# Windowed attention on one core: v of the last unit goes back to its usual place in the load order, and the first transfer is cut in two

## The chip, the cores and the metric

The kernel runs on one core of one Trainium2 chip. The metric is the device time of one execution in microseconds (us). A profiled execution also has a span, from its first to its last instruction, about 1.8 us shorter than its time.

## The reference

Attention inside windows of 64 rows, float32 in and out, 4 x 4096 rows of 1536 columns:

```python
q_w, k_w, v_w = (x.reshape(B, S // 64, 64, D) for x in (q, k, v))
logits = np.einsum('bnwd,bnud->bnwu', q_w, k_w) * D ** -0.5
attn = softmax(logits)                       # over the last axis
out = np.einsum('bnwu,bnud->bnwd', attn, v_w)
```

Each element of q, k and v is read once and each output written once: 301.99 MB in, 100.66 MB out.

## The kernel before

The rows are worked off in 32 units (`N = 32`) of 512 rows, numbered 0 to 31 here. A unit is four transfers of 3.146 MB on the HBM side: q, k and v in (cast from float32 to float16 on the way, so 1.573 MB land) and the result out. GpSimd issues them all, except the first load of q and the second half of the last store, which SyncE issues. Each operand is loaded into a landing buffer (`ql`, `kl`, two for v), copied by GpSimd to the buffer that TensorE reads (`q16`, `k16`, `v16`), and its landing buffer is then reloaded:

```python
def hand_over(src, dst, d, u, m, g):
    gp.wait_ge(d, 16 * u)                       # the load has landed
    gp.wait_ge(m, copies[0] // 3 + 1)           # the unit before no longer reads dst
    gp.tensor_copy(out=dst..., in_=src...).then_inc(c_l, 1)
    copies[0] += 1
    gp.wait_ge(c_l, copies[0])
    gp.sem_inc(g, 1)                            # TensorE may go on
```

The start, cut:

```python
raw = rows(qf, 0, SLOTS, SLOTS).rearrange("p h (r d) -> p (h r) d", d=D)
for sl, s in ((slice(0, 1), d_r0), (slice(1, 2), d_r1), (slice(2, SLOTS), d_r2)):
    nc.sync.dma_start(out=outs[0][:, sl, :], in_=raw[:, sl, :]).then_inc(s, 16)
...
nc.gpsimd.wait_ge(d_r0, 16)                     # holds back the loads behind it
nc.gpsimd.affine_select(out=ident[:, :], ...)   # the identity for the transposes
load("k", 0, k16, d_k0)
load("v", 0, v16, d_v0)
for i in range(SLOTS):                          # SLOTS = 4
    nc.gpsimd.wait_ge((d_r0, d_r1, d_r2, d_r2)[i], 16)
    nc.gpsimd.tensor_copy(out=q16[:, i, :], in_=outs[0][:, i, :])
    if i == 1:
        load("q", 1, ql, d_q)
load("k", 1, kl, d_k)
for u in range(1, NV + 1):                      # NV = 2
    load("v", u, vls[u % NV], d_v[u % NV])
```

GpSimd's main loop and the end of the program:

```python
for u in range(1, N):
    hand_over(ql, q16, d_q, u, m_q, g_q)
    if u + 1 < N:
        load("q", u + 1, ql, d_q)
    hand_over(kl, k16, d_k, u, m_k, g_k)
    if u + 1 < N:
        load("k", u + 1, kl, d_k)
    for what in {N - 3: "", N - 2: "-v"}.get(u, "s"):
        if what == "v":
            load("v", N - 1, vls[(N - 1) % NV], d_v[(N - 1) % NV])
        else:
            gp.wait_ge(m_q, u + 1)
            store(u - 2 if what == "-" else u - 1)
    if u == N - 2:
        store(u - 1)
    hand_over(vls[u % NV], v16, d_v[u % NV], (u + u % NV) // NV, m_v, g_v)
    if u + NV < N - 1:
        load("v", u + NV, vls[u % NV], d_v[u % NV])

base, o = (N - 1) * UR, outs[(N - 1) % NO]
for h, (eng, c) in enumerate(((gp, 1), (sy, 3))):   # the last store, in halves
    for a in range(2):
        eng.wait_ge(n_e[a], c)
    eng.dma_start(out=rows(of, base + R * P * h, R, R), in_=slots(o, R * h, R * h + R, R)).then_inc(d_l[h], 16)
gp.drain()
...                                             # SyncE waits for every store, then:
sy.sem_inc(done, 1)
gp.wait_ge(done, 1)
gp.sem_clear(range(lo, hi + 1))
```

So store 28 and v31 are held back until k31 has been issued, and the order at the end is q31, k31, store 28, v31, store 29, store 30, last store.

The softmax here doesn't subtract the row's maximum and nothing guards it: scores larger than these inputs give would overflow.

Of the kernel before, what the change touches and what calls it, by code (L numbers as in the profile page):

```python
# [17 lines left out]
def kernel(  # L18
# [13 lines left out]
    nc = tc.nc  # L32
    PE, DVE, ACT = (getattr(mybir.EngineType, e) for e in ("PE", "DVE", "Activation"))
    B, S, D = q.shape
    DC = D // (2 * P)
    NJ = D // 512
    SLOTS, R, H = 4, 2, 2
    UR = P * SLOTS
    N = B * S // UR
# [3 lines left out]
    def sb(name, shape, dtype):  # L43
        return ctx.enter_context(nc.sbuf_tensor(name, shape, dtype))
# [6 lines left out]
    def sem(name):  # L51
        sems.append(nc.alloc_semaphore(name))
        return sems[-1]
# [6 lines left out]
    NV = 2  # L60
    vls = [sb(f"vl{i}", [P, SLOTS, D], FP16) for i in range(NV)]
# [3 lines left out]
    outs = [sb(f"out{i}", [P, SLOTS, D], FP32) for i in range(NO)]  # L65
# [7 lines left out]
    ops = [ps(f"o{j}", [P, 512]) for j in range(NJ)]  # L73
    sp = ps("sp", [P, 4])

    d_r0, d_r1, d_r2, d_q, d_k, d_k0, d_v0 = (
        sem(n) for n in ("d_r0", "d_r1", "d_r2", "d_q", "d_k", "d_k0", "d_v0")
    )
    d_v = [sem(f"d_v{i + 1}") for i in range(NV)]
    d_o = [sem(f"d_o{i}") for i in range(NO)]  # L80
# [11 lines left out]
    m_q, m_k, m_v = (sem(n) for n in ("m_q", "m_k", "m_v"))  # L92
# [6 lines left out]
    def rows(x, row0, n, r):  # L99
        return x[row0 : row0 + P * n].rearrange("(h p r) d -> p h (r d)", p=P, r=r)  # L100

    def slots(t, lo, hi, r):
        return t[:, lo:hi, :].rearrange("p (h r) d -> p h (r d)", r=r)

    def load(name, u, dst, s):
        src = {"q": qf, "k": kf, "v": vf}[name]
        r = R if name == "v" else SLOTS
        nc.gpsimd.dma_start(
            out=slots(dst, 0, SLOTS, r), in_=rows(src, u * UR, SLOTS, r)
        ).then_inc(s, 16)  # L110
# [169 lines left out]
    def store(u):  # L280
        nc.gpsimd.dma_start(
            out=rows(of, u * UR, SLOTS, R), in_=slots(outs[u % NO], 0, SLOTS, R)
        ).then_inc(d_o[u % NO], 16)
# [3 lines left out]
    def hand_over(src, dst, d, u, m, g):  # L287

        gp = nc.gpsimd
        gp.wait_ge(d, 16 * u)  # L290
        gp.wait_ge(m, copies[0] // 3 + 1)
        gp.tensor_copy(  # L292
            out=dst[:, :, :].bitcast(FP32), in_=src[:, :, :].bitcast(FP32)
        ).then_inc(c_l, 1)
        copies[0] += 1
        gp.wait_ge(c_l, copies[0])
        gp.sem_inc(g, 1)

    with tc.tile_critical(no_gpsimd_drain=True):

        raw = rows(qf, 0, SLOTS, SLOTS).rearrange("p h (r d) -> p (h r) d", d=D)
        for sl, s in ((slice(0, 1), d_r0), (slice(1, 2), d_r1), (slice(2, SLOTS), d_r2)):
            nc.sync.dma_start(out=outs[0][:, sl, :], in_=raw[:, sl, :]).then_inc(s, 16)
        nc.vector.memset(ident[:, :], 0.0).then_inc(i_d, 1)
        nc.gpsimd.wait_ge(i_d, 1)
        nc.gpsimd.wait_ge(d_r0, 16)
        nc.gpsimd.affine_select(
            out=ident[:, :], in_=ident[:, :], compare_op=mybir.AluOpType.not_equal,
            fill=1.0, base=0, pattern=[[-1, P]], channel_multiplier=1,
        ).then_inc(i_p, 1)  # L310
        load("k", 0, k16, d_k0)
        load("v", 0, v16, d_v0)

        for i in range(SLOTS):
            nc.gpsimd.wait_ge((d_r0, d_r1, d_r2, d_r2)[i], 16)
            nc.gpsimd.tensor_copy(out=q16[:, i, :], in_=outs[0][:, i, :]).then_inc(c_q, 1)
            if i == 1:
                load("q", 1, ql, d_q)
        load("k", 1, kl, d_k)
        for u in range(1, NV + 1):  # L320
            load("v", u, vls[u % NV], d_v[u % NV])

        nc.vector.memset(ones[:, :], 1.0).then_inc(i_d, 1)
        nc.vector.memset(zeros[:, :], 0.0).then_inc(i_d, 1)
        for et in ets:
            nc.vector.memset(et[:, :, :, :], 0.0).then_inc(i_d, 1)
        nc.scalar.wait_ge(i_d, 5)
        nc.scalar.activation(zeros[:, 3:4], zeros[:, 0:1], EXP, bias=zeros[:, 0:1], scale=1.0)

        with nc.Fori(0, N, engines=OrderedEngineSet([PE]), head_slot={PE: 0}):  # L330
            tensor_unit()
        assert N % NO == 2
        for eng, unit in ((DVE, vector_unit), (ACT, scalar_unit)):
            with nc.Fori(0, N // NO, engines=OrderedEngineSet([eng]), head_slot={eng: 0}):
                for u in range(NO):
                    unit(u)
            for u in range(N - 2, N):
                unit(u)

        sy = nc.sync  # L340
        for j in range(NJ):
            for n in (2, 3):
                sy.sem_inc(f_o[j][n], 1)
        for a in range(2):
            sy.sem_inc(fr[a], NO)
        sy.wait_ge(i_p, 1)
        sy.wait_ge(i_d, 5)
        sy.wait_ge(c_q, SLOTS)
        sy.sem_inc(g_q, 1)
        sy.sem_inc(g_k, 1)._wait_ge(d_k0, 16)  # L350
        sy.sem_inc(g_v, 1)._wait_ge(d_v0, 16)
        for u in range(NO, N):
            sy.wait_ge(d_o[u % NO], 16 * (u // NO))
            for a in range(2):
                sy.sem_inc(fr[a], 1)

        gp = nc.gpsimd
# [5 lines that stand above are left out]
            if u + 1 < N:  # L363
                load("k", u + 1, kl, d_k)

            for what in {N - 3: "", N - 2: "-v"}.get(u, "s"):
                if what == "v":
                    load("v", N - 1, vls[(N - 1) % NV], d_v[(N - 1) % NV])
                else:
                    gp.wait_ge(m_q, u + 1)  # L370
                    store(u - 2 if what == "-" else u - 1)
            if u == N - 2:
                store(u - 1)
            hand_over(vls[u % NV], v16, d_v[u % NV], (u + u % NV) // NV, m_v, g_v)
            if u + NV < N - 1:
                load("v", u + NV, vls[u % NV], d_v[u % NV])

        base, o = (N - 1) * UR, outs[(N - 1) % NO]
        for h, (eng, c) in enumerate(((gp, 1), (sy, 3))):
            for a in range(2):  # L380
                eng.wait_ge(n_e[a], c)
            eng.dma_start(
                out=rows(of, base + R * P * h, R, R), in_=slots(o, R * h, R * h + R, R)
            ).then_inc(d_l[h], 16)
        gp.drain()
        for i in range(NO):
            last = max(u for u in range(N - 1) if u % NO == i)
            sy.wait_ge(d_o[i], 16 * (last // NO + 1))
        for i in range(2):
            sy.wait_ge(d_l[i], 16)  # L390
        sy.sem_inc(done, 1)
        gp.wait_ge(done, 1)
        lo, hi = min(s.num for s in sems), max(s.num for s in sems)
        assert hi - lo + 1 == len(sems)
        gp.sem_clear(range(lo, hi + 1))
# [30 lines left out]
```

## Time and profile before

| what | before |
|---|---|
| time, median of 4 runs (range) | 947.35 us (946.81 to 947.80) |
| span of the profiled execution | 946.4 us |
| one steady round of four transfers | 29.16 us, 431.5 GB/s |
| HBM traffic at that rate | 933.1 us |
| busy PE, DVE, ACT, GpSimd | 69%, 30%, 35%, 36% |
| DMA engines | full in 39 of the 40 slices |

(The prediction was made from the first three of these runs, median 947.6.) A transfer adds 16 to its semaphore, one step for each DMA engine, so the trace's semaphore records give 16 landing times for each. For the transfers around the gap, in us from the start of the span (worked out from the semaphore records of the kernel before):

```
transfer    issued    first engine done   last engine done
q30         855.98    878.8               881.7
k30         863.32    886.1               889.0
q31         885.13    894.6               896.3
k31         892.41    902.8               906.3
store 28    892.93    910.6               913.6
```

The engines are up to 3.5 us apart. A copy on GpSimd, and everything that waits for a transfer, sees only the last.

### The profile page before, as it was taken

How to read it: one execution, taken by the hardware profiler on the slowest of the kernel's cores; microseconds unless marked ns; L12 is line 12 of the kernel's file. 1: busy time of each engine (PE TensorE's matmuls, PEld its weight loads, DVE VectorE, ACT ScalarE, POOL GpSimd, SP SyncE). 2: the span in 40 equal slices, each digit the busy share in tenths (PEclk: the TensorE clock that was granted, in tenths of full speed). 3: DMA queues.
4: the chain of work that ended last, by engine and by line, in shares of the span. 5: the costliest groups of instructions: out<-in, count | busy, mean ns of one | idle time of the engine just before them, and what ended most of it. 6: DMA issues, size and time to landing. Idle time of an engine off the chain costs nothing. (4 is left out here: it accounts for less than half of the span.)

```text
span 946.4 us, 11421 instructions
## 1 busy us (share of the span) xinstructions
PE 651.0 (69%) x4096; PEld 419.8 (44%) x3456; DVE 279.7 (30%) x453; ACT 332.8 (35%) x642; POOL 341.5 (36%) x229
## 2 busy tenths in 40 slices
PE   2776866768667676667777667866768666777682
PEld 2544543445534345434554344543435533445450
DVE  1333223332233231333313323223322233232331
ACT  1433323333334342333423334323333234343252
POOL 4323343233442334423344323343233442333520
PEclk9989777897878887798878789878898879797897
DMA  9999999999999999999999999999999999999997
GB/s 250 216 229 270 283 281 282 242 257 283 281 280 258 243 282 282 278 270 236 278 282 280 279 238 265 282 280 282 249 251 283 283 281 264 238 279 283 197 315 321
DMA packets 26940, 253.35 MB, mean 268 GB/s; under 512 B 2096, under 2 KB 2096, under 8 KB 10544
## 3 DMA queue, kind: packets, MB, share of 16 engines
q0 software_dynamic: 26352, 248.52, 100.0%
q1 hardware_dynamic: 576, 4.72, 1.3%
q14 instruction: 10, 0.08, 0.0%
q8 instruction: 2, 0.03, 0.0%
HBM read 301.99 MB, written 100.66 MB: 425 GB/s over the span
## 5 line engine op out<-in xcount | busy, mean ns | idle before, releaser
L147 PE MATMUL tp<-ident,q 128*128 128x128 f32 x768 | 165.0, 384 | 185.6 <-PEq L213 172.7
L147 PEld LDWEIGHTS tp<-ident,q 128*128 128x128 f32 x768 | 131.2, 200 | 239.4 <-issue 236.8
L292 POOL COPY q<-ql 128x3072 f32<-128x3072 f32 x31 | 85.0, 2743 | 395.7 <-DMA ql<-in_q_dram 395.5
L159 PE MATMUL lt<-xq,xk 128*128 128x256 f16 x1536 | 210.2, 288 | 0.0
L147 PE MATMUL tp<-ident,k 128*128 128x128 f32 x768 | 136.3, 317 | 67.3 <-PEq L213 54.5
L159 PEld LDWEIGHTS lt<-xq,xk 128*128 128x128 f16 x1536 | 156.8, 102 | 30.4
L222 ACT COPY xq<-tp 128x512 f32<-128x512 f32 x96 | 60.2, 627 | 291.2 <-ACTq L213 291.2
L147 PEld LDWEIGHTS tp<-ident,k 128*128 128x128 f32 x768 | 105.1, 163 | 86.3 <-issue 83.9
L222 DVE COPY xq<-tp 128x512 f32<-128x512 f32 x96 | 66.4, 692 | 254.7 <-DVEq L213 254.7
L222 ACT COPY xk<-tp 128x512 f32<-128x512 f32 x96 | 59.8, 623 | 228.6 <-ACTq L213 228.6
L222 DVE COPY xk<-tp 128x512 f32<-128x512 f32 x96 | 66.5, 693 | 198.6 <-DVEq L213 198.6
L292 POOL COPY k<-kl 128x3072 f32<-128x3072 f32 x31 | 85.3, 2751 | 110.5 <-DMA kl<-in_k_dram 110.5
L264 ACT ACTIVATE et<-lt,zeros 32x128 f16<-32x128 f32 x256 | 92.0, 359 | 39.4 <-ACTq L213 36.1
L188 PEld LDWEIGHTS <-et 128*128 128x128 f16 x384 | 30.2, 97 | 152.7 <-issue 116.7
L115 PE MATMUL o<-v,et 128*128 128x512 f16 x384 | 93.3, 379 | 0.0
L251 DVE TENSOR_SCALAR out<-o,rs 128x512 f32<-128x512 f32 x128 | 90.2, 747 | 7.7
L292 POOL COPY v<-vl 128x3072 f32<-128x3072 f32 x31 | 85.5, 2758 | 10.4 <-DMA vl<-in_v_dram 10.4
L115 PE MATMUL tp<-v,et 128*128 128x512 f16 x256 | 75.8, 377 | 0.0
L241 DVE RECIPROCAL rs<-sp 128x2 f32<-128x2 f32 x64 | 10.6, 166 | 162.6 <-DVEq L213 162.4
L275 ACT ACTIVATE out<-tp,rs 128x512 f32<-128x512 f32 x64 | 44.0, 688 | 37.2 <-ACTq L213 31.3
L251 DVE TENSOR_SCALAR out<-tp,rs 128x512 f32<-128x512 f32 x64 | 48.1, 751 | 26.2 <-DVEq L213 26.2
L115 PE MATMUL lt<-v,et 128*128 128x512 f16 x128 | 48.3, 377 | 0.0
(22 smaller groups left out, 201.2 us busy)
## 6 DMA issues: line engine op xcount, KB each, us to landing
out_dram<-out POOLq DMA_DIRECT2D x31, 3072.0 KB, 32.5
ql<-in_q_dram POOLq DMA_DIRECT2D x31, 1536.0 KB, 25.8
kl<-in_k_dram POOLq DMA_DIRECT2D x31, 1536.0 KB, 25.8
vl<-in_v_dram POOLq DMA_DIRECT2D x31, 1536.0 KB, 35.7
out<-in_q_dram SPq DMA_DIRECT2D x2, 768.0 KB, 6.5
out<-in_q_dram SPq DMA_DIRECT2D x1, 1536.0 KB, 11.2
k<-in_k_dram POOLq DMA_DIRECT2D x1, 1536.0 KB, 12.2
v<-in_v_dram POOLq DMA_DIRECT2D x1, 1536.0 KB, 18.8
```

The costliest lines, as they stand in the source:

```text
L115: return nc.tensor.add_instruction(mybir.InstMatmult(name=nc.get_next_instruction_name(), engine=PE, ins=[low(rhs), low(w)], outs=[low(o)] ...
L147: ins = nc.tensor.transpose(tps[g % 2][:, r, j, :], pairs[:, c * P : (c + 1) * P], ident[:, :])
L159: ins = nc.tensor.matmul(lts[h][:, r, :, :], lhsT=halves(xk, c)[:, r, h, :, w], rhs=halves(xq, c)[:, :, h, :, w], start=(c == 0 and w == 0 ...
L188: ld = nc.tensor.ldweights(w)
L222: copy(out=dst, in_=tps[g % 2][:, :, :, :]).then_inc(f_c[g % 4], 1)
L241: ve.reciprocal(out=rs[:, n : n + R], in_=sp[:, n : n + R]).then_inc(n_d, 1)
L251: ins = ve.tensor_scalar_mul(scaled(u, n, j), bank(n, j), scalar1=rs[:, n : n + 1])
L264: ins = sc.activation(ets[h][s, :, :, s], lts[h][s, :, :, s], EXP, bias=zeros[s, 0:1], scale=scale)
L275: ins = sc.activation(scaled(u, n, j), bank(n, j), COPY, bias=0.0, scale=rs[:, n : n + 1])
L292: gp.tensor_copy(out=dst[:, :, :].bitcast(FP32), in_=src[:, :, :].bitcast(FP32)).then_inc(c_l, 1)
```

## The change

At the end, only store 28 is held back; v31 is loaded right after v of unit 29 has been handed over. At the start, the first slot of q comes in two halves.

```diff
...
-        for sl, s in ((slice(0, 1), d_r0), (slice(1, 2), d_r1), (slice(2, SLOTS), d_r2)):
-            nc.sync.dma_start(out=outs[0][:, sl, :], in_=raw[:, sl, :]).then_inc(s, 16)
+        for lo, hi, c0, c1, s in (
+            (0, 1, 0, D // 2, d_r0), (0, 1, D // 2, D, d_r1), (1, 2, 0, D, d_r2), (2, SLOTS, 0, D, d_r3)
+        ):
+            nc.sync.dma_start(
+                out=outs[0][:, lo:hi, c0:c1], in_=raw[:, lo:hi, c0:c1]
+            ).then_inc(s, 16)
...
-            nc.gpsimd.wait_ge((d_r0, d_r1, d_r2, d_r2)[i], 16)
+            nc.gpsimd.wait_ge((d_r1, d_r2, d_r3, d_r3)[i], 16)
...
-            for what in {N - 3: "", N - 2: "-v"}.get(u, "s"):
-                if what == "v":
-                    load("v", N - 1, vls[(N - 1) % NV], d_v[(N - 1) % NV])
-                else:
-                    gp.wait_ge(m_q, u + 1)
-                    store(u - 2 if what == "-" else u - 1)
-            if u == N - 2:
+            if u != N - 3:
+                gp.wait_ge(m_q, u + 1)
+                if u == N - 2:
+                    store(u - 2)
                 store(u - 1)
             hand_over(vls[u % NV], v16, d_v[u % NV], (u + u % NV) // NV, m_v, g_v)
-            if u + NV < N - 1:
+            if u + NV < N:
                 load("v", u + NV, vls[u % NV], d_v[u % NV])
```

The order at the end becomes v31, q31, k31, store 28, store 29, store 30, last store.

More of the change, by code (lines that the diff above doesn't have):

```diff
@@ L74 @@
     sp = ps("sp", [P, 4])
-    d_r0, d_r1, d_r2, d_q, d_k, d_k0, d_v0 = (
-        sem(n) for n in ("d_r0", "d_r1", "d_r2", "d_q", "d_k", "d_k0", "d_v0")
+    d_r0, d_r1, d_r2, d_r3, d_q, d_k, d_k0, d_v0 = (
+        sem(n) for n in ("d_r0", "d_r1", "d_r2", "d_r3", "d_q", "d_k", "d_k0", "d_v0")
     )
```

## The prediction

> **What bounds the kernel now.** I read the page first (busy shares, the 40 slices, bytes), then the timeline of GpSimd, which issues nearly all transfers, then the rate in 3 us windows at both ends, then landing times by tile. The page:
>
> ```profile
> span 946.4 us, 11421 instructions
> PE 651.0 (69%) x4096; PEld 419.8 (44%) x3456; DVE 279.7 (30%) x453; ACT 332.8 (35%) x642; POOL 341.5 (36%) x229
> DMA  9999999999999999999999999999999999999997
> HBM read 301.99 MB, written 100.66 MB: 425 GB/s over the span
> ```
>
> No compute engine is near full; the 16 DMA engines are, in every slice but the last. (The GB/s row counts a load that casts f32 to f16 at its f16 size, so about 215 there is a full-speed load and about 430 a full-speed store.) GpSimd's copies of q repeat at 735.98, 765.14 and 794.31 us, every 29.16 us, and one round moves four transfers (q, k, v, store) of 3.146 MB on the HBM side: 7.29 us each, 431.5 GB/s. So 402.65 MB need 933.1 us, and a change can win only part of the other 13.3: DMA time lost at the start, lost in between, or after the last byte. The diff touches start and end only. GpSimd's timeline of the end:
>
> ```profile
> 863.86 2.76 POOL L292 COPY v<-vl 128x3072 f32<-128x3072 f32 x1
> ...
> 885.13 0.53 POOL L108 DMA_DIRECT2D ql<-in_q_dram  x1 [0.58 <-POOL q L292]
> 889.07 2.75 POOL L292 COPY k<-kl 128x3072 f32<-128x3072 f32 x1 [3.41 <-DMA kl<-in_k_dram]
> 892.41 0.53 POOL L108 DMA_DIRECT2D kl<-in_k_dram  x1 [0.58 <-POOL k L292]
> 892.93 0.71 POOL L281 DMA_DIRECT2D out_dram<-out  x1
> 893.63 0.72 POOL L108 DMA_DIRECT2D vl<-in_v_dram  x1
> 894.35 0.71 POOL L281 DMA_DIRECT2D out_dram<-out  x1
> ...
> 906.36 2.75 POOL L292 COPY k<-kl 128x3072 f32<-128x3072 f32 x1 [5.57 <-DMA kl<-in_k_dram]
> 912.53 0.72 POOL L281 DMA_DIRECT2D out_dram<-out  x1 [3.42 <-ACTq L220]
> 920.93 2.74 POOL L292 COPY v<-vl 128x3072 f32<-128x3072 f32 x1 [7.69 <-DMA vl<-in_v_dram]
> 929.57 0.55 POOL L382 DMA_DIRECT2D out_dram<-out  x1 [5.89 <-ACT out L275]
> ```
>
> I number units 0 to 31. At 863.86 v of unit 29 is handed over and its buffer is free, but nothing is issued. The queue holds only q30 and k30, and when q31 goes in at 885.13, only the rest of k30 is ahead of it. The same stretch in 3 us windows (last column GB/s, before it the DMA share), against a full one ahead and behind:
>
> ```profile
> 875.00:878.00 3.00, 3.00 (x20) 0.51 (x6) 2.50 (x5) 2.03 (x5) 0.00 (x0) 1.00 1.04 221
> 884.00:887.00 3.00, 1.98 (x9) 1.64 (x10) 0.69 (x1) 0.05 (x1) 1.08 (x2) 0.50 1.05 197
> 887.00:890.00 3.00, 2.87 (x14) 2.31 (x15) 0.69 (x1) 1.20 (x2) 0.93 (x1) 0.59 0.91 188
> 893.00:896.00 3.00, 2.45 (x23) 2.06 (x21) 1.33 (x2) 0.76 (x2) 3.00 (x4) 1.00 0.96 168
> 896.00:899.00 3.00, 3.00 (x29) 2.69 (x28) 0.69 (x1) 0.87 (x2) 2.77 (x2) 1.00 0.92 175
> 932.00:935.00 3.00, 0.00 (x0) 0.00 (x0) 0.00 (x0) 0.00 (x0) 0.00 (x0) 0.81 1.00 426
> 941.00:944.00 3.00, 0.00 (x0) 0.00 (x0) 0.00 (x0) 0.00 (x0) 0.00 (x0) 0.50 0.03 12
> ```
>
> Loads ran at 168 to 197 instead of about 215: summed over one-microsecond windows from 885 to 902 the mean is 188, so 17 x (1 - 188/215) = about 2.1 us lost. From 920 to 940 all is full. The landing times of the q load show the thin queue:
>
> ```profile
> DMA to landing us min/median/max: 11.2/25.8/26.4
> ```
>
> A load normally lands 25.8 us after issue, 3.5 transfers, so 2.5 were ahead of it. The 11.2 is q31: half a transfer ahead of it.
>
> **What the Trainium skill says.** The page "DMA: Bandwidth & Descriptors", section "Specifications", gives a fabric ceiling of 435 GB/s; the steady rounds run at 431.5, so they have nothing more to give. Its section "Issuing engines are not separate DMA queues" says that transfers of all issuers share the same 16 engines and interleave: reordering creates no bandwidth, it can only fill gaps. Its section "Why a DMA increments its semaphore by 16 and not by 1" says the 16 engines finish independently: a transfer lands with its slowest engine, and an engine that is ahead idles when nothing is queued behind. The profile gives only the mean of the engines; the dips at 885 and 894 fit, but don't prove it. "Anatomy of one DMA" puts a fixed 2.0 us beside the data time, most of it write receipt; here the rate falls at about 940.5 and the last store lands at 929.57 + 13.3 (median of its issue row) = 942.9, so it agrees.
>
> **The change, part by part.** (1) End, removed and moved: v31 leaves its place between two stores and is issued as usual, right after the hand-over of v29, at about 867. Store 28 and store 29 go out behind k31 at about 893, store 30 as before. No instruction or byte is added here. From the landing of k30 at 889.07, with both orders at 7.29 us each:
> Before, from the landings: q31 896.3, k31 906.3, store 28 913.6, v31 920.8, store 29 928.3, store 30 936.4, last unit 942.9. That is 53.8 us for seven transfers; 7 x 7.29 = 51.0, so 2.8 us were lost, and 10.0 - 7.3 = 2.7 of them lie at k31, where the windows dip.
> After: v31 896.4, q31 903.7, k31 911.0, store 28 918.2, store 29 925.5, store 30 932.8, last unit 940.1. A whole transfer (v31) now stands between k30 and q31, and no dip should stay. Best case -2.8 us.
>
> (2) What this does to the last unit. k31 lands 4.7 us later, v31 24 us earlier. The 7.7 us wait for v31 vanishes and k31 becomes the gate. From unit 29: k lands 859.97, its transposes start 863.03, the third of four output rows is ready at 878.0 (14.97 later), the last at 879.5. So the first half of the last store is issued at 911.0 + 3.1 + 15.0 + 0.3 = 929.4, the other half at about 930.9: nearly where it was (929.57, 930.57). But the DMA has caught up: store 30's data end at 932.8 less about 2 of receipt, 930.8, and the first bytes of a store issued at 929.4 flow after 0.55 of issuing and about 1 us, at about 930.9. Margin before: about 3.5 us. Margin after: about zero. I charge 0.5 us.
>
> (3) Output buffers: unit 31 writes the buffer that store 28 reads. Store 28 lands 918.2 instead of 913.6; unit 31 first writes at 911.0 + 3.1 + 11.4 = 925.5. Still hidden, by 7 us.
>
> (4) Start: GpSimd's wait at the start now ends with half a row slot.
>
> ```profile
> 6.98 0.28 POOL L307 TENSOR_SCALAR_AFFINE_SELECT ident<-ident 128x128 f32<-128x128 f32 x1 [6.54 <-DMA out<-in_q_dram]
> 7.51 0.68 POOL L108 DMA_DIRECT2D k<-in_k_dram  x1 [0.24 <-issue]
> ...
> 3.00:6.00 3.00, 0.00 (x0) 0.00 (x0) 0.00 (x0) 0.00 (x0) 0.00 (x0) 1.00 0.96 371
> 6.00:9.00 3.00, 0.00 (x0) 0.00 (x0) 0.00 (x0) 0.00 (x0) 1.77 (x4) 1.00 1.06 449
> ```
>
> Bytes at the windows' rates: 0.79 MB are moved by about 4.7 us, half of it by about 3.7, so the identity and k0 start about 1.0 us earlier. But the queue is full at that time (449 in 6 to 9) with q's other slots until about 9.7, and k0 issued at 7.51 is in time. So this only makes k0 overlap more of q: hidden, except for a small weakness at 9.5 to 10 us (369, then mixed), which I put at 0.2 us. The price is one more issue on SP, 1.33/3 = 0.44 us, while the first piece moves: hidden too.
>
> Sum: -2.8 + 0.3 (part of the dip stays) + 0.5 - 0.2 = -2.2 us; 947.6 - 2.2 = 945.4 us.
>
> **The rivals.** (A) The compute of the last unit becomes the bound of the end: k31 a transfer later, and the final halves come when the DMA has run dry. For it: the zero margin of step 2; any delay of k31 or a lower granted clock (0.50 to 0.59 in two windows above) lengthens the chain. Against it: the same compute is done with the same durations. It would give back 1 to 2.5 us: 946.5 to 948. (B) The dip at 885 to 902 isn't the thin queue but something of that moment: four transfers described in a row on GpSimd beside a copy (893 to 899). Then it stays, and the time is 947.0 to 947.6. Against it: the first dip, at 885 to 890, has only one issue in it. (C) The start counts in full, because everything behind it is in order on the DMA: 1.0 us more, 944.4. Against it: no idle DMA window between 3 and 12 us.
>
> **Range and chances.** 2% are 19 us; everything outside the DMA floor is 13.3 us, so faster by over 2% would need the floor to fall: 0.01. Slower by 19 us would take a stall of two and a half transfers, such as a last unit blocked behind store 28, which has 7 us in hand: 0.01. The range comes from the rivals and from 0.7 us of spread in the times: A or B at their worst give 948.0, C with the whole 2.8 gives 943.8.
>
> **What would show it.** Right: the q31 load lands about 18.5 us after issue instead of 11.2 (minimum of its row), v's wait of 7.7 us is gone, windows 885 to 902 at 210 or more, k31 lands near 911, the last halves are issued at 929 to 931, the last store lands near 940.5, the affine select starts near 6.0. Wrong: a DMA share well below 1 at 929 to 933 (A), the dips in place with v31 queued (B), q1's hand-over a full microsecond before 34.36 (C), or a total over 948.

## The result

The changed kernel takes 943.41 us (median of 4 runs, 943.15 to 944.48) against 947.35 us: ratio 0.9961, 95% interval 0.9944 to 0.9978. The gain of 3.9 us is clear and well within 2%. The time lies 0.4 us below the predicted range of 943.8 to 948.0, and the gain was forecast at 2.2 us.

The page of the changed kernel:

```profile
span 942.7 us, 11422 instructions
HBM read 301.99 MB, written 100.66 MB: 427 GB/s over the span
```

The bytes are the same, they just took less time. GpSimd's timeline of the end:

```profile
866.72 0.71 POOL L108 DMA_DIRECT2D vl<-in_v_dram  x1 [0.60 <-POOL v L292]
881.33 2.75 POOL L292 COPY q<-ql 128x3072 f32<-128x3072 f32 x1 [13.90 <-DMA ql<-in_q_dram]
884.66 0.56 POOL L108 DMA_DIRECT2D ql<-in_q_dram  x1 [0.58 <-POOL q L292]
...
892.50 1.43 POOL L281 DMA_DIRECT2D out_dram<-out  x2
...
910.53 2.75 POOL L292 COPY k<-kl 128x3072 f32<-128x3072 f32 x1 [4.60 <-DMA kl<-in_k_dram]
...
914.59 2.76 POOL L292 COPY v<-vl 128x3072 f32<-128x3072 f32 x1
929.31 0.57 POOL L385 DMA_DIRECT2D out_dram<-out  x1 [11.97 <-ACT out L275]
```

v31 now goes out at 866.72 instead of 893.63, and its copy at 914.59 waits for nothing, where it waited 7.69 us before. k31 is copied 4.2 us later than before (910.53 for 906.36), yet the last store is issued at the same time (929.31 for 929.57). In the windows that dipped before (last column GB/s, a full load stretch is about 215):

```profile
884.00:887.00 3.00, 2.44 (x11) 2.10 (x12) 0.69 (x1) 0.52 (x1) 0.64 (x2) 0.50 0.96 203
887.00:890.00 3.00, 2.87 (x14) 2.41 (x13) 0.89 (x2) 0.74 (x2) 1.35 (x1) 0.51 1.02 211
893.00:896.00 3.00, 2.65 (x13) 2.14 (x14) 0.90 (x2) 0.56 (x1) 3.00 (x3) 0.56 1.16 244
896.00:899.00 3.00, 3.00 (x25) 2.71 (x24) 0.56 (x1) 0.61 (x1) 0.69 (x1) 0.87 0.95 203
```

They carry 203 to 244 (212 in the mean from 885 to 902) instead of 168 to 197. The landing times of the q load confirm it:

```profile
DMA to landing us min/median/max: 18.5/25.8/26.2
```

The shortest, q31, is 18.5 us where it was 11.2.

Where the 3.7 us between the two spans lie, marked at the hand-over of k30 and at the last landing of any store: the program up to k30 took 889.07 us before and 888.65 after; from k30 to the last landing 53.80 and 51.92; from the last landing to the end 3.50 and 2.13. The middle part was predicted. The last part was not in the prediction at all, and it became the main question of the experiments.

### The profile page after: what moved, and what is told of

Read it like the earlier page. It is cut to its first block, busy times and chain, and to the rows that moved or that the text cites. A ratio compares the mean times of both kernels' runs of the same rounds, so it can differ in the third digit from the quotient of the medians.

```text
span 942.7 us, 11422 instructions
## 1 busy us (share of the span) xinstructions
PE 650.6 (69%) x4096; PEld 419.1 (44%) x3456; DVE 279.7 (30%) x453; ACT 332.6 (35%) x642; POOL 341.5 (36%) x229
```

## The experiments

**Two theories of the end.** Theory D: GpSimd's `drain` at the end waits for its own stores, then takes some 2 us more, and only then can the final clear run; so it matters which engine issued the store that lands last. Before, GpSimd's half landed last (942.87, SyncE's 942.0); after the change it landed ahead of SyncE's (939.20 and 940.57). Rival E: the end follows the last landing by a fixed time. The rivals of the prediction are tested too: B (the dip comes from GpSimd's burst of issues), C (the start counts in full), and the claim of a margin of about zero behind A. Dropping the drain outright was not tried on the chip; the drain was instead given less to wait for.

### The change again: a_again

No edit.

> The changed kernel again, for a second profile and a tighter ratio. Theory D (the end is set by GpSimd's drain, which in both profiles ends 2.24 us after GpSimd's own last store landed; in the change that store lands 1.4 us ahead of SyncE's, before it landed 0.9 us behind): ratio to before 0.9955 to 0.997, about 943.4 us, and the drain again ends about 2.2 us after GpSimd's last store landed. Theory S (the profiled start, where q's last slots landed at 15.9 us instead of 13.0, is a matter of chance): the last slots of q land at 13 to 14 us this time and q of unit 1 is handed over near 34.4; if it is the half slot that does it, again near 15.9 and 35.0.

Measured: 943.68 us (943.22 to 945.96, 5 runs) against 946.77; ratio 0.9967 (0.9953 to 0.998). The result holds. Its profiled execution was its slowest, 945.96, and shows why: GpSimd's half of the last store had one DMA engine far behind (first engine 934.3, last 940.7), so the drain ended only at 942.94. q's last slots landed at 15.7 us, so that is not chance: it comes with the half slot.

### The end alone: tail_only

```diff
 # start as before; of the change, only the main loop
```

> The end of the change alone, the start as before. If the whole gain comes from the end (theory D with the thin queue): 943.0 to 943.5 us, as fast as or up to 0.7 us faster than the whole change. If the start carries part of it (rival C of the prediction, 1 us): 944.4 or more.

Measured: 944.26 us (943.79 to 944.90); ratio to before 0.9972 (0.9959 to 0.9986). That is 2.5 us of the 3.1 us that the whole change won. It is 0.8 us slower than the upper end of what the theory gave, and short of the 944.4 that rival C asked for; the intervals of the two ratios overlap for the most part. In its profile GpSimd's half landed at 937.7, SyncE's at 941.3, and the drain was over in time; the last compute was late for another reason (see fill_store).

### The start alone: head_only

```diff
 # start as changed; the main loop as before
```

> The start of the change alone, the end as before. If the start is hidden or hurts: 947.2 to 948.1, with q of unit 1 handed over at 34.3 to 35.1 us. Rival C (it counts in full): 946.4, handed over near 33.4.

Measured: 946.99 us (946.18 to 948.17) against 946.77; ratio 1.0002 (0.9989 to 1.0016). q of unit 1 was handed over at 34.55 us, before at 34.36. The start by itself wins nothing that can be seen.

### Before, with SyncE issuing both halves: before_sp

```diff
-        for h, (eng, c) in enumerate(((gp, 1), (sy, 3))):
+        for h, (eng, c) in enumerate(((sy, 1), (sy, 3))):
```

> The kernel before with both halves of the last store issued by SyncE, nothing else. The last bytes land at the same time, about 942.9 us. Theory D: GpSimd's drain then waits only for store 30 (landed 936.5), and the program ends about 2 us after the last landing instead of 3.5: gain 1.3 to 2.0 us, about 945.6. Rival E (the end is a fixed 3.5 us after the last landing, whoever issued it, as the prediction took it): 947.0 to 947.7.

Measured: 945.34 us (944.13 to 946.04) against 946.77; ratio 0.9981 (0.9967 to 0.9994). A gain of 1.4 us from changing nothing but the issuer of one half store, as theory D asks and E excludes. Its last landing came 53.29 us after k30, nearly as before (53.80), but the program ended 1.33 us after it, not 3.50.

### The other transfer in the gap: fill_store

```diff
-            for what in {N - 3: "", N - 2: "-v"}.get(u, "s"):
+            for what in {N - 2: "vs"}.get(u, "s"):
 ...
-            if u == N - 2:
-                store(u - 1)
```

> The kernel before with the other transfer in the gap: store 28 goes out at its usual place (about 864) and v31 stays held, behind k31, ahead of store 29. GpSimd's burst of three issues beside a copy stays. Thin-queue theory: it doesn't matter what fills the gap; q31 and k31 land about 18.5 us after issue (before 11.2 and 13.9), no windows under 200 at 885 to 902, and the time is that of the end change alone, 943.5 to 944.5. Rival B (GpSimd's burst of issues makes the dip): dip stays, 946.5 or more. Rival V (v31 must come early, its wait of 7.7 us was on the path): 946 or more, with a wait for v.

Measured: 944.98 us (944.28 to 946.00) against 947.16; ratio 0.9975 (0.9961 to 0.9988). With v31 still held back, but store 28 in the gap, the gain is that of the end alone (0.9972). The landing times of its q and of its k load:

```profile
DMA to landing us min/median/max: 18.5/25.8/27.1
DMA to landing us min/median/max: 18.9/25.8/27.2
```

The minima, q31 and k31, were 11.2 and 13.9 before. GpSimd still issued three transfers in a row at 892.6 to 894.5, beside the copy of v, and nothing dipped at 893:

```profile
893.00:896.00 3.00, 2.45 (x23) 2.08 (x21) 1.38 (x2) 0.63 (x1) 3.00 (x4) 1.00 1.05 320
```

A burst of issues by itself makes no dip, so rival B falls as it was put. (Whether the burst added to the second dip of the kernel before is not separated: by its packet records the first engine was through with q31 at 894.3, 1.9 us after k31 had been issued, and yet the 16 engines were idle for 0.5 us in the mean between 894 and 900.) The thought that v31 had to come early falls too: its copy, after a wait of 2.9 us, was done at 921.3, and the products that need it began at 926.79, after the exponentials. What counts is that something stands between k30 and q31.

The last store, though, was issued at 932.50, 21.0 us after k31's copy began, where the change took 18.8. The windows with the transposes of k31 and with the end of store 30 tell why (the third figure from the right is the granted TensorE clock, then the DMA share); first the change, then fill_store:

```profile
915.00:920.00 5.00, 4.53 (x41) 4.16 (x42) 1.71 (x3) 1.25 (x2) 2.34 (x1) 1.00 1.00 425
930.00:935.00 5.00, 0.00 (x0) 0.00 (x0) 0.29 (x1) 0.00 (x0) 0.00 (x0) 0.93 0.97 410
```

```profile
915.00:920.00 5.00, 4.87 (x24) 3.95 (x23) 1.39 (x2) 0.62 (x1) 2.06 (x2) 0.50 1.02 371
930.00:935.00 5.00, 2.35 (x12) 0.29 (x3) 3.02 (x6) 2.10 (x4) 0.57 (x1) 0.94 0.49 206
```

With the clock granted at 0.50 instead of 1.00 the chain behind k31 came some 2 us later, and the DMA engines ran half empty at 930 to 935. The clock was 0.66 to 0.69 at 915 to 920 in the profiles of tail_only, after_sp and tail_sp_nowait too (issue 19.1 to 19.8 us after k31, share at 930 to 935 of 0.71 to 0.83), and 1.00 in the other five of the new order (18.5 to 19.1 us, share 0.91 to 1.01). From the packet records, the DMA engines were idle between 924 and 936 for 2.5 us in fill_store (mean of the 16), for 1.2 to 1.6 us in those three and for 0.3 to 0.5 us in the five. In the order of before, head_only had a lowered clock at 926 to 929 and no idle time (0.03 us). So the margin of about zero shows as idle DMA. A cost in time is not shown for the three: their last landing came 51.3 to 51.6 us after k30, that of the five 51.2 to 52.5 (table below). Only fill_store's is late, 52.96.

### Nothing held back: no_hold

```diff
-            for what in {N - 3: "", N - 2: "-v"}.get(u, "s"):
...
+            gp.wait_ge(m_q, u + 1)
+            store(u - 1)
             hand_over(vls[u % NV], v16, d_v[u % NV], (u + u % NV) // NV, m_v, g_v)
-            if u + NV < N - 1:
+            if u + NV < N:
                 load("v", u + NV, vls[u % NV], d_v[u % NV])
```

> The kernel before with nothing held back: stores 28, 29, 30 and v31 all at their usual places, so two transfers stand between k30 and q31. No dip, but k31 lands a transfer later than in the change, near 918, and the last halves are issued near 937 while the queue has run dry near 931: an idle DMA of some 6 us. If the margin of the change was about zero, as predicted: 949 to 951 us (7 us over the change). If the order of the stores doesn't matter because the DMA is the only bound: 943.5 to 944.5.

Measured: 950.06 us (949.48 to 951.36) against 947.16; ratio 1.0028 (1.0013 to 1.0044). Slower than either kernel, as expected. GpSimd's timeline and the windows around the last compute:

```profile
919.17 2.75 POOL L292 COPY k<-kl 128x3072 f32<-128x3072 f32 x1 [4.49 <-DMA kl<-in_k_dram]
...
937.71 0.54 POOL L376 DMA_DIRECT2D out_dram<-out  x1 [11.67 <-ACT out L275]
```

```profile
929.00:932.00 3.00, 2.26 (x20) 1.68 (x18) 0.00 (x0) 1.81 (x6) 0.00 (x0) 1.00 0.77 328
932.00:935.00 3.00, 2.99 (x20) 0.65 (x9) 1.33 (x3) 2.82 (x7) 0.00 (x0) 1.00 0.06 25
935.00:938.00 3.00, 2.56 (x13) 0.29 (x3) 2.54 (x6) 2.03 (x4) 0.29 (x1) 1.00 0.00 0
```

With one transfer more ahead of k31, the last compute ends at about 938, and the DMA engines stand idle waiting for it: 3 x (0.23 + 0.94 + 1.00) = 6.5 us in these nine. So there is room for exactly one transfer ahead of q31: none leaves the queue thin, one fits, two starve its end.

### The change, with SyncE issuing both halves: after_sp

```diff
-        for h, (eng, c) in enumerate(((gp, 1), (sy, 3))):
+        for h, (eng, c) in enumerate(((sy, 1), (sy, 3))):
```

> The changed kernel with both halves of the last store issued by SyncE. Theory D (GpSimd's drain ends 2.24 us after its own last landing and in the change still ends 0.8 us after SyncE is done): 0.5 to 1.2 us faster than the change, 942.4 to 943.1, and the drain ends before the last landing. Rival E (no such thing): as the change, 943.4 to 943.7.

Measured: 943.21 us (943.06 to 943.86) against 947.16; ratio 0.9957 (0.9943 to 0.9970). A miss in size: by the medians no more than 0.2 to 0.5 us under the change's 943.41 and 943.68, by the ratios to the kernel before 0.4 to 0.9 us, and either way inside the intervals. I had taken the profiled execution of the change, in which the drain was late by 0.8 us, for the usual one. It was the slowest of its four. What the drain costs the change in a usual run is under 1 us and not told from zero.

### The change, with the issuers exchanged: after_swap

```diff
-        for h, (eng, c) in enumerate(((gp, 1), (sy, 3))):
+        for h, (eng, c) in enumerate(((sy, 1), (gp, 3))):
```

> The changed kernel with the issuers exchanged: SyncE issues the first half of the last store, GpSimd the second. Same bytes, same order of readiness. Theory D: GpSimd's own last store is now the very last to land, so the whole 2.24 us come after the last landing: 1 to 2 us slower than the change, 944.6 to 945.6. Rival E: as the change, 943.4 to 943.9.

Measured: 945.75 us (945.52 to 947.40) against 947.16; ratio 0.9990 (0.9976 to 1.0003). The same bytes in the same order, 2.1 to 2.3 us slower than the change and 2.5 us slower than after_sp, slightly more than expected: GpSimd's store is now the last to land (940.25), the drain ends at 942.51, the program at 943.75. With the order of the change, but the drain behind the last landing, most of the gain is gone.

### The start, with the drain out of the way: tail_sp and after_sp_b

tail_sp is tail_only with SyncE issuing both halves; after_sp_b is after_sp again.

> The end of the change, with both halves of the last store issued by SyncE (so GpSimd's drain is out of the way), and the start of before. Beside after_sp_b on the same chip it isolates the start. Start hidden (as predicted, 0.2 us at most): within 0.5 us of after_sp_b, 942.8 to 943.8. Start counts (rival C, up to 1 us): 0.7 to 1.2 us slower than after_sp_b.

> The changed kernel with both halves issued by SyncE, again, for the comparison with tail_sp: 943.0 to 943.5; q's last slots land near 16 us as in every run with the half slot so far, against 13.0 to 13.4 with the start of before.

Measured: tail_sp 944.13 us (943.67 to 944.60), ratio 0.9959 (0.9945 to 0.9972); after_sp_b 943.58 us (943.25 to 944.87), ratio 0.9951 (0.9937 to 0.9964); the kernel before was at 948.05 with a wide range, 946.57 to 949.55. The start makes a difference of 0.55 us, between the two expectations. It has the same sign and size as between tail_only and a_again (0.6 us), but both lie within the intervals, and head_only alone shows 0.2 us the other way.

### GpSimd's first wait taken away: tail_sp_nowait

```diff
-        nc.gpsimd.wait_ge(d_r0, 16)
         nc.gpsimd.affine_select(
```

> As tail_sp, but GpSimd doesn't wait for any piece of q before the identity, k0 and v0 (the identity needs only the zeroed tile, each cast still waits for its own slot, so this is free of races): k0 is issued near 1.5 us instead of 7.5. If the DMA is full from 2 us on, whatever is issued (start hidden): the same as tail_sp within 0.7 us, at best 0.8 us faster from a steeper ramp between 2 and 3.5 us. If the early issue of k0 counts: 3 us or more faster. If k0 and v0 in front of q's slots hold up the first unit: slower, with the first hand-over of q later than 35 us.

Measured: 943.50 us (943.05 to 943.67); ratio 0.9950 (0.9936 to 0.9963), 0.6 us under tail_sp, within its intervals. GpSimd's timeline of its start:

```profile
1.99 0.68 POOL L108 DMA_DIRECT2D k<-in_k_dram  x1 [0.24 <-issue]
...
21.81 2.87 POOL L315 CAST q<-out 128x1536 f16<-128x1536 f32 x2 [6.72 <-DMA out<-in_q_dram]
24.62 0.54 POOL L108 DMA_DIRECT2D kl<-in_k_dram  x1
...
34.09 2.75 POOL L292 COPY q<-ql 128x3072 f32<-128x3072 f32 x1 [7.50 <-DMA ql<-in_q_dram]
```

k0 is issued 5.5 us sooner than before (1.99 for 7.51), the load of k1 8.7 us later (24.62 for 15.91), and q of unit 1 is handed over 0.3 us sooner than before (34.09 for 34.36). Order at the start hardly matters: the DMA share from 3 to 12 us is 0.99 to 1.10 here and was 0.96 to 1.06 before, so the engines are busy either way. With head_only, that speaks against rival C: the start doesn't count in full.

### The end in all profiles

Worked out from the records of the profiled executions: the semaphore steps of the stores, and GpSimd's drain, which starts just before its last issue and is not counted as busy time on the page. Times from the start of the span in us; k30 is the hand-over of k30.

```
kernel           k30 to last   GpSimd's last   drain   drain minus   last landing
                 landing       landing         ended   that landing  to end
before           53.80         942.87          945.13  2.26          3.50
head_only        53.84         942.63          944.89  2.26          2.60
before_sp        53.29         937.21          939.43  2.22          1.33
after            51.92         939.20          941.46  2.26          2.13
a_again          52.48         940.68          942.94  2.26          3.05
tail_only        51.47         937.72          939.98  2.26          1.34
after_sp         51.29         933.27          935.49  2.22          1.34
after_swap       51.15         940.25          942.51  2.26          3.50
tail_sp          51.98         933.14          935.36  2.22          1.33
after_sp_b       52.49         934.89          937.11  2.22          1.34
tail_sp_nowait   51.58         933.24          935.46  2.22          1.33
fill_store       52.96         937.88          940.14  2.26          1.34
no_hold          57.41         943.06          945.32  2.26          1.34
```

One rule covers all 13: the drain ends 2.22 to 2.26 us after GpSimd's own last store has landed, and the program ends 1.24 us after the drain or 1.34 us after the last landing of all, whichever is later. The order of before takes 53.6 us from k30 to the last landing (mean of the first three rows), that of the change 51.8 (mean of the eight rows from after to tail_sp_nowait): 1.8 us.

## Why the prediction was wrong, and where it was right

**Right: the bound and the dip.** The DMA engines bound the kernel, the stretch at 885 to 902 was short of work, and a transfer ahead of q31 fills it. fill_store shows that it is the depth of the queue and not v, and not GpSimd's burst alone. How the thin queue costs time can be seen in the table of landings in the section on before and in the trace's packet records (start, duration and bytes of each piece that a DMA engine moved): the first DMA engine was through with k30 at 885.8, the last only at 888.7; q31 was issued at 885.13, and its first packet started at about 886.4. Between 886.0 and 886.5 only 10 packets were moving on the 16 engines, where it is 16 in a full stretch. But idle engines, which the prediction named, are the smaller part. Summed over 885 to 902 the packets give 2.25 us lost, as forecast (2.1); 0.77 us of it is idle engines, and the rest is packets of q31 and k31 that took up to 1.9 and 2.4 us instead of 0.93. In the change the same stretch loses 0.05 us, with no idle engine. Why the first packets after a pause are slow is not shown.

**Wrong, without weight: the 2 us of receipt.** The prediction read the fall of the rate at about 940.5 and the landing at 942.9 as the skill's 2 us of fixed time, most of it write receipt. The packet records show one late engine moving data until 942.52; the landing followed 0.35 us later. In the 13 profiles the last landing of all follows the last data packet by 0.34 to 0.47 us. A store on an empty queue had its first packet 1.1 us after the start of its issue (fill_store, no_hold), not 1.55 as in step 2. Store 30's data thus ended, engine by engine, at about 929.5 to 932.4, and the first bytes of the last store could flow at 930.4. The two errors nearly cancel: the idle time at 924 to 936 was 0.4 us in the profile of the change, where 0.5 was charged.

**Right: the last unit.** k31 landed at 910.5 (forecast 911.0), the halves were issued at 929.31 and 930.34 (929.4 and about 930.9), the last store landed at 940.57 (near 940.5). no_hold shows that the margin was really used up: with one transfer more the DMA engines starve. The prediction's two charges, 0.3 for a rest of the dip and 0.5 for the end, made its gain on this stretch 2.0 us; the profiles show 1.8.

**Wrong: a term was missing from the sum.** This is the step that failed. The prediction named three places for time outside the DMA floor: lost at the start, in between, or "after the last byte". It worked out the first two and left the third out of its sum, so the 3.5 us from the last landing (942.9) to the end of the span was carried over unseen. It isn't constant. It was 3.5 us because GpSimd's half store landed last and the drain came on top of it. The change moved k31 and the last compute against store 30, so that the DMA had nearly caught up when the halves were issued: GpSimd's half started at once, a microsecond ahead of SyncE's, and landed first, 1.4 us ahead in the profile of the change, 0.5 us in that of a_again and 3.6 us in that of tail_only. Before, both halves stood behind store 30. In the profile of before one late engine put GpSimd's half last, 0.9 us behind SyncE's; in that of head_only, which has the same end, it landed 0.9 us ahead, and the drain still set the end. By the rule above GpSimd's half must land 2.2 us ahead for the drain to cost nothing. Beyond the 1.34 us that follow any last landing, the drain added 2.2 and 1.3 us in these two profiles, 0.8 and 1.7 us in the two of the change and nothing in tail_only. So its cost varies between executions, and that the new order makes the lead longer is seen in these few profiles, not tested by itself. before_sp measures what the drain cost before, 1.4 us; after_sp, what it still costs, 0.2 to 0.9 us, not told from zero. So about 1.8 us of queue and about 1 us of drain are found, 2.8 of the 3.1 to 3.9 us; the drain's share carries the intervals of two ratios, over 1 us each way.

**Wrong, without weight: the start.** Step 4 had the first half slot landing a microsecond sooner. Its first 15 engines did (3.5 to 4.2 us, against 4.8 to 5.9 for the whole slot), but the sixteenth landed at 6.6 instead of 6.7, so the identity came at 6.90 instead of 6.98. And q's last slots came at 15.4 to 16.8 us in every profile with the half slot, and at 13.0 to 13.4 in those without (the one without the wait aside), which the prediction did not foresee. Neither moved the time, as it said. Some 0.5 us between the starts, seen in two pairs and not in a third, stays open; it would close the sum, but it is not shown.

**The rivals.** A (the compute becomes the bound of the end) came in part: the four profiles with a lowered clock show idle DMA, of which only fill_store's is seen in its last landing. It was one transfer away from coming in full (no_hold). B as it was put fell by fill_store; C is not borne out by head_only and tail_sp_nowait, though a start worth some 0.5 us stays possible.

**A better version?** after_sp is in no way slower than the change, and its end doesn't depend on a late DMA engine in GpSimd's half; its gain over the change is within the intervals. Nothing tried is clearly faster than the change.

## What to carry to other kernels

In a kernel bound by DMA, look at the depth of the queue at every place where the order of issue departs from the steady round: here a single transfer in flight cost 2 us, one more ahead was right, and two more starved the end. When pricing a change near the end, write out the time from the last landing to the last instruction as its own term and ask which wait sets it. A store that is to land last is best issued by an engine that has no drain behind it.

## What the Trainium skill lacked or had wrong

- How long GpSimd's drain takes behind its own DMAs is on no page: 2.22 to 2.26 us after the last of them has landed, in all 13 profiles; a store landing last cost 1.4 us when GpSimd had issued it instead of SyncE (before_sp).
- "DMA: Bandwidth & Descriptors", section "Why a DMA increments its semaphore by 16 and not by 1", says that the engines finish independently, which the trace shows, but not how far apart: 1.5 to 3.5 us for most loads and stores here, and 6.3 us for one half store (934.3 to 940.7 in a_again).
- No page says that cutting a transfer in two can leave its slowest engine where it was: with the half slot, 15 engines landed at 3.5 to 4.2 us and one at 6.6, against 6.7 for the last engine of the whole slot.
- "DMA: Bandwidth & Descriptors", section "Anatomy of one DMA", cited in the prediction, gives most of its fixed 2.0 us to the write receipt. The total is not far off here: a half store on an empty queue landed 5.3 to 5.4 us after its issue (no_hold, fill_store), of which its 1.573 MB take 3.6 at the steady rate, which leaves 1.7. But by the packet records 1.1 us of it pass before the first packet and 0.3 to 0.5 after the last.
